# Feed-forward up-projections of a hybrid decoder step: blocks of two by two in seven products

## The chip, the cores and the metric

One Trainium2 chip, one core. The metric is the device time of one launch in microseconds (us), the median of several runs. PE is TensorE (matmuls), PEld its weight loads, DVE is VectorE, ACT is ScalarE, POOL is GpSimd, SP is SyncE (it issues the loads here).

## What is computed

One step of two layers over 512 prompt tokens and 64 sample tokens, model width 1024, all in float32. Each layer is a mixer (pools and a gated delta rule in the first, a short gated convolution in the second) and a gated feed-forward of width 2816. The change is in the feed-forward:

```python
def conv_ffn(h, buf, w_up, conv_w, w_down):
    up = h @ w_up
    gate, val = up[..., :D_FF], up[..., D_FF:]
    gc, new_buf = causal_dwconv(gate, buf, conv_w)   # 3 taps
    return (jax.nn.silu(gc) * val) @ w_down, new_buf
```

`h` is the RMS norm of `x` with a weight per channel; its factor per token is applied behind the product.

## The kernel before, in words

Activations lie with channels on the partitions: 8 tiles of 128 channels by 2 halves of 288 columns (256 prompt tokens and 32 sample tokens each). Every float32 product is made of three: an operand is split into a rounded high part and a low part (the rest), and PE adds high x high, high x low and low x high in one accumulation. `gemm` (L212) does that for one tile of 128 outputs: for each k-tile of 128 channels six matmuls of 288 columns, three for each half of the tokens (L227, L229, L231), into an accumulator of two PSUM banks (`acc2`, two of them).

`Feed` (L76) brings the weights in the order of use: a DMA from SP into `raw` (two buffers of 128 x 1024), the high part by ACT (L111), the low part by DVE (L113; for some tiles of the first mixer by POOL), into `wh` and `wl` (two buffers each). `get` (L117) keeps it as far ahead as the buffers allow.

`ffn` (L1044) runs in two halves of 11 tiles of the feed-forward width. For each tile: the gate product of 8 k-tiles (48 matmuls), `ext_mul` (L260, L262) scales it into `e`, which has two earlier columns in front and the states of the samples (`ext_halo`, `ext_state`: POOL copies at L249, L266, L267); `conv` (L269) is one tap on ACT (L271) and two on DVE (L273); silu on ACT (L1062); times `rE`, the norm's factor, on DVE (L1063). Then the value product (48 matmuls), the gated product by `ext_to_t` (L279, L281), and `split_hl` makes its high part on ACT (L284) and its low part on DVE (L285) in `gh`, `gl`. After 11 tiles come the 8 down products, each over 11 k-tiles, added to `x` by `residual` (L343).

At the end of a product that makes a new `x`, `norm_operand` (L287) makes the split operand of the next one and `norm_sum` (L293) adds up squares; `norm_end` (L317) runs from a hook after five k-steps of the next product and puts two small matmuls for each half into PE's queue. `last` (L1085) does the last two down products by halves of the tokens.

The order on each engine is not written out: a scheduler orders the instructions by their place in the program and by when their operands are ready in its own reckoning, and gives out buffers and semaphores; on the chip each engine then runs its list in that fixed order.

Of the kernel before, what the change touches and what calls it, by code (L numbers as in the profile page):

```python
# [8 lines left out]
F = mybir.dt.float32  # L9
R = mybir.dt.float32r  # L10
# [7 lines left out]
KD = D // 128  # L18
# [56 lines left out]

class Feed:  # L76
    """Weights of the products in the order in which they are used: loaded ahead and split into two parts."""

    def __init__(self, tc, pool, units):
        self.tc, self.nc, self.pool, self.units = tc, tc.nc, pool, units  # L80
        self.raw, self.hl = {}, {}
        self.nd = self.ns = self.n = 0
        self.between = None
        self.slow = ()

    def cuts(self, i, w):
        """the first in halves, for an early start"""
        return ((0, 512), (512, w)) if i == 0 else ((0, w),)

    def load(self, upto):  # L90
        while self.nd < min(upto, len(self.units)):
            src, w = self.units[self.nd]
            t = self.pool.tile([128, 1024], F, tag="raw", name="raw", bufs=RAWB)
            for a, b in self.cuts(self.nd, w):
                self.nc.sync.dma_start(out=t[:, a:b], in_=src[:, a:b])
                if self.between and self.nd == 0 and a == 0:
                    self.between()
            self.raw[self.nd] = t
            self.nd += 1

    def split(self, upto):
        while self.ns < min(upto, len(self.units)):
            self.load(self.ns + 1)
            t = self.raw.pop(self.ns)
            w = self.units[self.ns][1]
            if self.ns < len(self.units) - 2:
                h, l = (self.pool.tile([128, 1024], R, tag=n, name=n, bufs=HLB) for n in ("wh", "wl"))
            else:
                h, l = (self.extra.tile([128, 768], R, tag=n, name=n, bufs=2) for n in ("eh", "el"))
            for a, b in self.cuts(self.ns, w):  # L110
                self.nc.scalar.activation(out=h[:, a:b], in_=t[:, a:b], func=AF.Copy)  # L111
                e = self.nc.gpsimd if self.ns in self.slow else self.nc.vector
                e.tensor_tensor(out=l[:, a:b], in0=t[:, a:b], in1=h[:, a:b].bitcast(F), op=SUB)  # L113
            self.hl[self.ns] = (h, l)
            self.ns += 1

    def get(self):  # L117
        i = self.n
        self.n += 1
        self.split(i + HLB)  # L120
        self.load(i + HLB + RAWB)
        return self.hl.pop(i)
# [10 lines left out]
LY = (4, 8)  # L133
# [8 lines left out]
RAWB, HLB, WB = 2, 2, 6  # L142


def body(ctx, tc, I, O):
# [9 lines left out]
    wk = pool(ctx, "wk")  # L155
    xm = pool(ctx, "xm")
    ps = pool(ctx, "ps", space=PSUM)

    cst = com.tile([128, NCST], F, name="cst")
    vec = com.tile([128, NVEC], F, name="vec")  # L160

    def C(name, rows=128):
        o, w = CST[name]
        return cst[0:rows, o:o + w]
# [9 lines left out]
    def W(name="w"):  # L174
        return wk.tile([128, 711], F, tag="w", name=name, bufs=WB)
# [7 lines left out]
    units = []  # L183
    for c in ORD.split():
        if c != "g":
            units.append((I["w_in_ab"][{"p": 0, "q": 4, "k": 8, "v": 12, "z": 16}[c[0]] + int(c[1])], 1024))
    for m in range(8):
        units.append((I["w_out_ab"][m], 1024))

    def ffn_units(l):  # L190
        for half in range(2):
            for f in range(half * HF, half * HF + HF):
                units.append((I["w_up"][l, f], 1024))
                units.append((I["w_up"][l, NF + f], 1024))
            for m in range(8):
                k0 = half * HF
                units.append((I["w_down"][l, m][:, k0 * 128:(k0 + 6) * 128], 768))
                units.append((I["w_down"][l, m][:, (k0 + 6) * 128:(k0 + 11) * 128], 640))

    ffn_units(0)  # L200
    for m in range(8):
        for j in (1, 2, 0):
            units.append((I["w_in_c"][j * 8 + m], 1024))
    for m in range(8):
        units.append((I["w_out_c"][m], 1024))
    ffn_units(1)
    feed = Feed(tc, wts, units)
# [3 lines left out]
    # ---------------------------------------------------------------- pieces  # L211
    def gemm(out, H, L, kmap, nks):  # L212
        """out[:, c] (+)= W.T @ x over the k-tiles of one accumulation, in the order kmap; nks: k-tiles per unit"""
        tot = sum(nks)
        oc = out if isinstance(out, list) else [out[:, 0], out[:, 1]]
        i = k0 = 0
        for nk in nks:
            h, l = feed.get()
            for _ in range(nk):
                k = kmap[i]  # L220
                kk = k - k0
                wh = h[:, kk * 128:(kk + 1) * 128]
                wl = l[:, kk * 128:(kk + 1) * 128]
                st, sp = i == 0, i == tot - 1
                xh, xl = (H[k], L[k]) if isinstance(H, list) else (H[:, k], L[:, k])
                for c in range(2):
                    PE.matmul(out=oc[c][:, 0:288], lhsT=wh, rhs=xh[:, c, :], start=st, stop=False)  # L227
                for c in range(2):
                    PE.matmul(out=oc[c][:, 0:288], lhsT=wh, rhs=xl[:, c, :], start=False, stop=False)  # L229
                for c in range(2):  # L230
                    PE.matmul(out=oc[c][:, 0:288], lhsT=wl, rhs=xh[:, c, :], start=False, stop=sp)  # L231
                i += 1
                yield
            k0 += nk
# [16 lines left out]
    def ext_mul(e, h, a, b):  # L251
        """e's data columns = a * b, both [128, 2, >=288] by token columns"""
# [24 lines left out]
    def ext_to_t(dst, c, h, b):  # L277
        """dst [128, 2, 288] = outputs of a convolution (columns of c) * b"""
# [8 lines left out]
    def norm_operand(x, xh, xl, k, nw):  # L287
        """x [128, 2, 288] * w, split: the operand of the next product but for the factor of a token"""
# [28 lines left out]
    def norm_end(rE=None):  # L317
        h = wk.tile([128, 576], R, tag="w", name="acch", bufs=WB)
        l = wk.tile([128, 576], R, tag="w", name="accl", bufs=WB)
# [25 lines left out]
    # ---------------------------------------------------------------- start: operand and norm of the first layer  # L345
    xwh = ops.tile([128, KD, 2, 288], R, tag="xh", name="xwh")
    xwl = ops.tile([128, KD, 2, 288], R, tag="xl", name="xwl")
# [15 lines left out]
    feed.load(1)  # L363
    start(3)
    feed.load(2)
    start(KD)
    nc.sync.dma_start(out=cst, in_=I["cst"])
    for k in range(KD):
        norm_operand(xs[k], xwh, xwl, k, ("nmix", 0))
        feed.split(min(k + 1, 2))  # L370
# [4 lines left out]
    # ---------------------------------------------------------------- first mixer: pools and gated delta  # L375
# [6 lines left out]
    late = pool(ctx, "late")  # L382
# [956 lines left out]
```

## Time and profile before

| | |
|---|---|
| median of 3 runs | 1386.51 us (1386.44 to 1387.59) |
| span of the profiled execution, first to last instruction | 1381.5 us |
| median less span | 5.0 us |
| matmuls (all, with the small ones) | 9996 |
| granted TensorE clock, mean | 0.977 |

The profile is one execution on one core. The time of that execution is listed nowhere by itself; in the sums its own time is taken as its span and the 5.0 us around it. A line of the groups reads: source line, engine, operation, output <- inputs by tile name, shapes, count, busy time, mean of one in ns, idle time before it and what ended that. The timeline reads: start in us, duration in us, engine, line, operation, and in brackets the idle time before it with its releaser. A matmul's duration is its whole passage, and the next one starts before it ends; the pace is read from the starts or from the count.

### The profile page before, as it was taken

Reading aid. Unit: us, or ns where it says so; the run is one execution under the profiler, and the core shown is the slowest. Engines: PE = TensorE matmul, PEld = TensorE weight load, DVE = VectorE, ACT = ScalarE, POOL = GpSimd, SP = SyncE. Lnnn points to the kernel's source line nnn. Section 1 sums busy time; section 2 is a strip of 40 time slices with the busy share of each in tenths; the row PEclk is TensorE's granted clock in tenths of the full one; section 3 lists DMA queues with packets and bytes.
Section 4 is the critical chain, followed back from the end, with each engine's and each line's share of the span. In section 5 each row is a group of like instructions: output and inputs, shape, how many; then the busy total and the mean of one; then the engine's idle time right before and its main releaser. Section 6 shows DMA issues by size and latency. Waiting matters only on the chain.

```text
span 1381.5 us, 23767 instructions
## 1 busy us (share of the span) xinstructions
PE 1348.7 (98%) x9996; PEld 1325.1 (96%) x9996; DVE 760.6 (55%) x1260; ACT 500.1 (36%) x781; POOL 174.0 (13%) x316
## 2 busy tenths in 40 slices
PE   8898999899999999999999999999999999999997
PEld 7788789899999999999999999999999999999997
DVE  7669537986555324555446454456655423555434
ACT  6463326655333212333334222234333212333333
POOL 2123112201111001111000011000111000111000
PEclk9889779999999999999999999999999999999999
DMA  5111122362222232222232222222222233222232
GB/s 200 43 40 59 40 62 76 98 191 84 77 92 74 73 85 92 92 77 82 81 84 98 80 77 92 79 85 84 77 92 79 74 84 102 77 82 88 70 84 90
DMA packets 51081, 117.37 MB, mean 85 GB/s; under 512 B 5280, under 2 KB 22048, under 8 KB 50976
## 3 DMA queue, kind: packets, MB, share of 16 engines
q1 hardware_dynamic: 50976, 115.87, 26.3%
q8 instruction: 78, 1.28, 0.4%
q14 instruction: 27, 0.22, 0.1%
HBM read 110.21 MB, written 5.64 MB: 84 GB/s over the span
## 4 chain that ended last, share of the span: by engine, by line
PE 87%; DVE 8%; ACT 3%; issue 2%; DMA 0%; SPq 0%; POOLq 0%; POOL 0%; ACTq 0%
PE mm L231 27%; PE mm L227 27%; PE mm L229 27%; DVE c L273 2%; PE mm L1108 1%; DVE Xb L690 1%; DVE tm L688 1%; PE kqs L925 1%; PE mp L731 0%; PE up L867 0%; PE kk L649 0%; ACT xwh L290 0%; ACT wh L111 0%; DMA x<-in_x_dram 0%; DVE t L311 0%
## 5 line engine op out<-in xcount | busy, mean ns | idle before, releaser
L111 ACT ACTIVATE wh<-raw 128x1024 fp32r<-128x1024 f32 (+2 forms) x211 | 206.1, 977 | 613.3 <-PE mm L229 553.1
L227 PE MATMUL mm<-xh,wh 128*128 128x288 f32 x1792 | 382.7, 295 | 0.0
L231 PE MATMUL mm<-xh,wl 128*128 128x288 f32 x1792 | 382.7, 295 | 0.0
L229 PE MATMUL mm<-xl,wh 128*128 128x288 f32 x1792 | 382.4, 295 | 0.0
L227 PEld LDWEIGHTS mm<-xh,wh 128*128 128x128 f32 x1792 | 288.0, 188 | 0.2 <-issue 0.2
L231 PEld LDWEIGHTS mm<-xh,wl 128*128 128x128 f32 x1792 | 288.0, 188 | 0.0
L229 PEld LDWEIGHTS mm<-xl,wh 128*128 128x128 f32 x1792 | 288.0, 188 | 0.0
L113 DVE TENSOR_TENSOR wl<-raw,wh 128x1024 fp32r<-128x1024 f32 (+2 forms) x193 | 214.4, 1111 | 110.1 <-ACT wh L111 105.7
L231 PE MATMUL mm<-gh,wl 128*128 128x288 f32 x788 | 169.2, 296 | 0.0
L229 PE MATMUL mm<-gl,wh 128*128 128x288 f32 x788 | 169.1, 296 | 0.0
L227 PE MATMUL mm<-gh,wh 128*128 128x288 f32 x788 | 169.1, 296 | 0.0
L227 PEld LDWEIGHTS mm<-gh,wh 128*128 128x128 f32 x788 | 127.3, 189 | 0.0
L231 PEld LDWEIGHTS mm<-gh,wl 128*128 128x128 f32 x788 | 127.3, 189 | 0.0
L229 PEld LDWEIGHTS mm<-gl,wh 128*128 128x128 f32 x788 | 127.3, 189 | 0.0
L273 DVE SCALAR_TENSOR_TENSOR c<-e,vec,c 128x592 f32<-128x592 f32 (+1 forms) x140 | 121.7, 872 | 7.7 <-ACT c L271 5.4
L260 DVE TENSOR_TENSOR e<-mm,rT 128x512 f32<-128x512 f32 x59 | 40.7, 691 | 152.9 <-PE mm L231 152.4
L266 POOL COPY nfp<-e 128x2 f32<-128x2 f32 x44 | 11.3, 257 | 629.9 <-DVE e L260 629.9
L227 PE MATMUL mm<-xwh,wh 128*128 128x288 f32 x304 | 77.5, 330 | 6.4 <-ACT wh L111 6.4
L229 PE MATMUL mm<-xwl,wh 128*128 128x288 f32 x304 | 77.3, 329 | 0.0
L231 PE MATMUL mm<-xwh,wl 128*128 128x288 f32 x304 | 77.1, 329 | 0.0
L279 DVE TENSOR_TENSOR g<-c,mm 128x512 f32<-128x512 f32 x52 | 35.8, 688 | 63.3 <-PE mm L231 63.2
L227 PEld LDWEIGHTS mm<-xwh,wh 128*128 128x128 f32 x304 | 55.5, 209 | 7.2 <-ACT wh L111 6.7
(362 smaller groups left out, 1457.6 us busy)
## 6 DMA issues: line engine op xcount, KB each, us to landing
raw<-in_w_up_dram SPq DMA_DIRECT2D x88, 512.0 KB, 3.2
raw<-in_w_down_dram SPq DMA_DIRECT2D x32, 384.0 KB, 3.1
raw<-in_w_in_c_dram SPq DMA_DIRECT2D x24, 512.0 KB, 3.2
raw<-in_w_down_dram SPq DMA_DIRECT2D x32, 320.0 KB, 2.9
raw<-in_w_in_ab_dram SPq DMA_DIRECT2D x19, 512.0 KB, 3.2
hss<-in_state_dn_dram SPq DMA_DIRECT2D x16, 256.0 KB, 3.0
raw<-in_w_out_ab_dram SPq DMA_DIRECT2D x8, 512.0 KB, 3.4
raw<-in_w_out_c_dram SPq DMA_DIRECT2D x8, 512.0 KB, 3.2
```

Source lines behind the costliest of these rows:

```text
L111: self.nc.scalar.activation(out=h[:, a:b], in_=t[:, a:b], func=AF.Copy)
L113: e.tensor_tensor(out=l[:, a:b], in0=t[:, a:b], in1=h[:, a:b].bitcast(F), op=SUB)
L227: PE.matmul(out=oc[c][:, 0:288], lhsT=wh, rhs=xh[:, c, :], start=st, stop=False)
L229: PE.matmul(out=oc[c][:, 0:288], lhsT=wh, rhs=xl[:, c, :], start=False, stop=False)
L231: PE.matmul(out=oc[c][:, 0:288], lhsT=wl, rhs=xh[:, c, :], start=False, stop=sp)
L260: V.tensor_tensor(out=P2(e[:, h:h + PT]), in0=a[:, :, 0:256], in1=b[:, :, 0:256], op=MUL)
L273: V.scalar_tensor_tensor(out=c[:, 0:n], in0=e[:, j:j + n], scalar=vcol(vname, idx * (h + 1) + j), in1=c[:, 0:n], op0=MUL, op1=ADD)
L279: V.tensor_tensor(out=dst[:, :, 0:256], in0=P2(c[:, 0:PT]), in1=b[:, :, 0:256], op=MUL)
L688: V.tensor_tensor(out=tv, in0=lv.to_broadcast([128, a, b]), in1=xv.to_broadcast([128, a, b]), op=MUL)
L690: V.tensor_tensor(out=uv, in0=uv, in1=tv, op=ADD)
L925: PE.matmul(out=kq[:, h * 128:(h + 1) * 128], lhsT=km[:, b].rearrange("p i t -> p (i t)"), rhs=t[:, s], start=b == 0, stop=b == 7)
L1108: PE.matmul(out=o[m][:, c, 0:288], lhsT=a[:, w], rhs=b[:, k, c], start=k == i == 0, stop=k == HF - 1 and i == 2)
```

## The change

The up-projection of a feed-forward tile is taken as a product of blocks: rows gate and value (128 outputs each), inner dimension in two halves of 4 k-tiles, columns in the two halves of the tokens. Seven products of sums of blocks take the place of eight. Weight sums (`add`) are made on GpSimd, four additions of 128 x 512 for a tile; the sums of activations (`form_operand`) on VectorE when the operand is made, with their split. A tile thus has the weight units raw (1024 columns), two sums (1024 each) and a half block (512, its low part on GpSimd). The products are chained through two PSUM banks and a third (`b`), with copies to SBUF by ACT in between; the last two products of a tile run among those of the next (`sevens`). `Gated` has the work behind the products: half of the gate's scaling and the product with `rE` go to GpSimd, the state copies to ACT. The feed-forward runs in three passes of 8, 7 and 7 tiles instead of two of 11, and out projections make their tiles in the order 0 4 1 5 2 6 3 7. The number of buffers changes from the feed-forward on: 4 `raw`, 3 pairs of `wh` and `wl`, 2 pairs of 512 columns, 3 of sums, 7 work tiles of 594 columns; some tiles of the mixer and the constants move to other places.

```diff
 class Feed:
...
+    def pairs(self, srcs):
+        prev = None
+        for t in [*srcs, None]:
+            if t is not None:
+                r, g = len(self.loads), len(self.groups)
+                self.loads += [(t[0], 1024, 4), (t[1], 1024, 3)]
+                self.groups.append(r)
+                self.plan += [("raw", r, 1024), ("sum", g, 1)]
+            if prev is not None:
+                self.plan.append(("one", prev + 1, 512))
+            if t is not None:
+                self.plan.append(("sum", g, 0))
+                prev = r
...
+    def add(self):
+        g = self.ng
+        if g == len(self.groups) or self.groups[g] + 1 >= self.nl or self.sgs.places() < 2:
+            return False
...
+        add = lambda out, x, y: self.nc.gpsimd.tensor_tensor(out=out, in0=x, in1=y, op=ADD)
+        add(t0[:, lo], b[:, lo], b[:, hi])
+        add(t1[:, lo], t0[:, lo], a[:, lo])
+        add(t1[:, hi], a[:, lo], b[:, lo])
+        add(t0[:, hi], t1[:, lo], a[:, hi])
...
+    def split(self):
...
+        for a, b in self.cuts(self.ns, w):
+            self.nc.scalar.activation(out=h[:, a:b], in_=src[:, a:b], func=AF.Copy)
+            e = self.nc.gpsimd if kind == "one" or kind == "raw" and n in self.slow else self.nc.vector
+            e.tensor_tensor(out=l[:, a:b], in0=src[:, a:b], in1=h[:, a:b].bitcast(F), op=SUB)
...
+    def ahead(self):
+        while self.load() or self.add() or self.split():
+            pass
...
+RAWX, HLX, HL1, SGB, WX = 2, 1, 2, 3, 7
+PASS = ((0, 8), (8, 7), (15, 7))
+PAIR = (0, 4, 1, 5, 2, 6, 3, 7)
...
+    def sevens(tiles, ops):
+        fa, fb, ft = ops
+        x11, x21, x22 = ([t[:, i] for i in range(2)] for t in (fa, fb[:, :, :, 0], fb[:, :, :, 1]))
+        d1, t3, d2, t4 = ([ft[:, i, :, n] for i in range(2)] for n in range(4))
+
+        def product(o, u, half, x, first, last):
+            h, l = u[2:]
+            xh, xl = x
+            for j in range(4):
+                w = slice(half * 512 + j * 128, half * 512 + j * 128 + 128)
+                for i, (a, b) in enumerate(((h, xh), (h, xl), (l, xh))):
+                    PE.matmul(out=o[:, 0:288], lhsT=a[:, w], rhs=b[:, j], start=first and j == i == 0,
+                              stop=last and j == 3 and i == 2, skip_group_check=True)
+                yield
+        prev = None
+        for t in [*tiles, None]:
+            if t is not None:
+                o, b, sv = acc2(), bank("b"), W("sv")
+                p, q = o[:, 0], o[:, 1]
+                t.begin()
+                u = feed.take()
+                yield from product(p, u, 0, x11, True, False)
+                S.activation(out=sv[:, 0:288], in_=p[:, 0:288], func=AF.Copy)
+                yield from product(b, u, 1, x21, True, True)
+                feed.done(u)
+                t.c11(sv[:, 0:288], b[:, 0:288])
+            if prev is not None:
+                was, p0, q0, sv0, u = prev
+                yield from product(p0, u, 1, x22, False, True)
+                feed.done(u)
+                was.c12(p0[:, 0:288])
+            if t is not None:
+                u1 = feed.take()
+                yield from product(p, u1, 0, d2, False, False)
+                S.activation(out=sv[:, 288:576], in_=p[:, 0:288], func=AF.Copy)
+            if prev is not None:
+                u = feed.take()
+                yield from product(q0, u, 0, t4, False, True)
+                feed.done(u)
+                was.c21(sv0[:, 288:576], q0[:, 0:288])
+            if t is not None:
+                yield from product(q, u1, 1, t3, True, False)
+                feed.done(u1)
+                u = feed.take()
+                yield from product(p, u, 0, d1, False, False)
+                t.c22(p[:, 0:288], q[:, 0:288])
+                prev = (t, p, q, sv, u)
...
+    def form_operand(x, F3, m, nw, half):
...
+        S.activation(out=P2(xw[:, 0:576]), in_=x, func=AF.Copy, scale=w)
+        j = m % 4
+        if m < 4:
+            S.activation(out=fa[:, 0, j], in_=xw[:, 0:288], func=AF.Copy)
+            V.tensor_tensor(out=fa[:, 1, j], in0=xw[:, 0:288], in1=fa[:, 0, j].bitcast(F), op=SUB)
+            half[j] = xw
+            return
+        S.activation(out=fb[:, 0, j], in_=P2(xw[:, 0:576]), func=AF.Copy)
+        V.tensor_tensor(out=fb[:, 1, j], in0=P2(xw[:, 0:576]), in1=fb[:, 0, j].bitcast(F), op=SUB)
...
+        for i in range(2):
+            d = W("fd")
+            d1, t = d[:, 0:288], d[:, 288:576]
+            if i == 0:
+                V.tensor_tensor(out=d1, in0=y[:, 0:288], in1=y[:, 288:576], op=SUB)
+                V.tensor_tensor(out=t, in0=xw[:, 288:576], in1=y[:, 288:576], op=SUB)
+                d0 = d1
+            else:
+                V.scalar_tensor_tensor(out=d1, in0=d0, scalar=-1.0, in1=xw[:, 288:576], op0=MUL, op1=SUB)
+                V.scalar_tensor_tensor(out=t, in0=d1, scalar=-1.0, in1=xw[:, 0:288], op0=MUL, op1=SUB)
+            split_hl(ft[:, 0, j, 2 * i:2 * i + 2], ft[:, 1, j, 2 * i:2 * i + 2], P2(d[:, 0:576]))
...
+    class Gated:
...
+        def half(self, on, c, a):
+            e = self.e
+            es = smp(e[:, 2 + PT:2 + PT + 80], 2)
+            on.tensor_tensor(out=e[:, 2 + 256 * c:258 + 256 * c], in0=a[:, 0:256], in1=rT[:, c, 0:256], op=MUL)
+            on.tensor_tensor(out=es[:, c, :, 2:10], in0=a[:, 256:288].rearrange("p (s t) -> p s t", s=4),
+                             in1=rT[:, c, 256:288].rearrange("p (s t) -> p s t", s=4), op=MUL)
+        def c11(self, a, b):
+            V.tensor_tensor(out=self.v[:, 0:288], in0=b, in1=a, op=ADD)
+            self.half(G, 0, self.v[:, 0:288])
+        def c12(self, a):
+            self.half(V, 1, a)
+            e = self.e
+            c = self.c = W("c")
+            n = conv(e, c, 2, "cff", self.l * 66 // 3 + self.f)
+            S.activation(out=self.sp[:, self.f], in_=e[:, PT:PT + 2], func=AF.Copy)
+            S.activation(out=self.ss[:, self.f], in_=self.es[:, :, 8:10], func=AF.Copy)
+            S.activation(out=c[:, 0:n], in_=c[:, 0:n], func=AF.Silu)
+            G.tensor_tensor(out=c[:, 0:n], in0=c[:, 0:n], in1=rE[:, 0:n], op=MUL)
+        def c22(self, a, b):
+            S.activation(out=self.v[:, 288:576], in_=a, func=AF.Copy, scale=-1.0)
+            V.tensor_tensor(out=self.v[:, 288:576], in0=self.v[:, 288:576], in1=b, op=SUB)
+        def c21(self, a, b):
+            V.scalar_tensor_tensor(out=self.v[:, 0:288], in0=b, scalar=-1.0, in1=a, op0=MUL, op1=SUB)
...
+            ext_to_t(P2(t[:, 0:576]), self.c, 2, v)
+            split_hl(*self.g, P2(t[:, 0:576]))
...
     def ffn(l, nw):
...
-        for half in range(2):
+        for f0, n in PASS:
             gh, gl = gtiles()
...
+            yield from sevens([Gated(l, f0 + j, st, sp, ss, gh, gl, j) for j in range(n)], ops_)
...
+                yield from gemm(o, gh, gl, range(n))
```

## Rows read from the trace of the kernel before

**Rows 1.** The page, busy time, share of the span and instructions of each engine.
```profile
PE 1348.7 (98%) x9996; PEld 1325.1 (96%) x9996; DVE 760.6 (55%) x1260; ACT 500.1 (36%) x781; POOL 174.0 (13%) x316
```
**Rows 2.** The page, the chain that ended last, by engine.
```profile
PE 87%; DVE 8%; ACT 3%; issue 2%; DMA 0%; SPq 0%; POOLq 0%; POOL 0%; ACTq 0%
```
**Rows 3.** Windows: busy us (count) of PE, PEld, DVE, ACT, POOL; clock, DMA share, GB/s.
```profile
400.00:500.00 100.00, 100.00 (x752) 100.00 (x752) 44.81 (x62) 27.44 (x34) 10.51 (x20) 1.00 0.26 79
440.72:453.50 12.78, 12.78 (x98) 12.78 (x97) 7.15 (x10) 4.30 (x5) 2.16 (x4) 1.00 0.21 58
```
**Rows 4.** Timeline of DVE behind two results of the last product.
```profile
1354.26 0.46 DVE L1111 TENSOR_TENSOR xr<-xr,mm 128x288 f32<-128x288 f32 x1 [1.16 <-PE mm L1108]
...
1358.66 0.45 DVE L1111 TENSOR_TENSOR xr<-xr,mm 128x288 f32<-128x288 f32 x1 [2.43 <-PE mm L1108]
```
**Rows 5.** Groups of instructions, shapes apart: POOL, DVE, ACT.
```profile
L113 POOL TENSOR_TENSOR wl<-raw,wh 128x1024 fp32r<-128x1024 f32 x18 | 43.2, 2402 | 113.8 <-ACT wh L111 77.0 <-PE mm L231 30.3 <-ACT Vb_s L759 6.5
L1164 POOL TENSOR_TENSOR y<-xr,rb 128x288 f32<-128x288 f32 x2 | 1.6, 792 | 83.8 <-ACT rb L1163 83.8
...
L113 DVE TENSOR_TENSOR wl<-raw,wh 128x1024 fp32r<-128x1024 f32 x129 | 158.0, 1225 | 21.2 <-ACT wh L111 16.7 <-issue 0.2
L273 DVE SCALAR_TENSOR_TENSOR c<-e,vec,c 128x592 f32<-128x592 f32 x104 | 86.5, 832 | 3.9 <-ACT c L271 1.8
L285 DVE TENSOR_TENSOR gl<-g,gh 128x576 fp32r<-128x576 f32 x52 | 39.1, 752 | 4.5 <-ACT gh L284 4.5
L279 DVE TENSOR_TENSOR g<-c,mm 128x512 f32<-128x512 f32 x52 | 35.8, 688 | 63.3 <-PE mm L231 63.2
L281 DVE TENSOR_TENSOR g<-c,mm 128x64 f32<-128x64 f32 x52 | 11.4, 220 | 1.6
...
L111 ACT ACTIVATE wh<-raw 128x1024 fp32r<-128x1024 f32 x147 | 155.7, 1059 | 418.2 <-PE mm L229 373.5 <-issue 44.3 <-PE mm L231 0.2
L271 ACT ACTIVATE c<-e,vec 128x592 f32<-128x592 f32 x52 | 41.2, 792 | 5.4 <-DVE e L262 1.3
L284 ACT ACTIVATE gh<-g 128x576 fp32r<-128x576 f32 x52 | 35.7, 687 | 14.2 <-DVE g L281 7.9
L1062 ACT ACTIVATE c<-c 128x592 f32<-128x592 f32 x44 | 30.8, 699 | 84.6 <-DVE c L273 84.5
L290 ACT ACTIVATE xh<-x,vec 128x576 fp32r<-128x576 f32 x12 | 9.3, 775 | 2.7 <-DVE x L1019 1.4 <-DVE x L343 1.2
```
**Rows 6.** Timeline of DVE, two places in the first mixer, one in the feed-forward.
```profile
57.19 2.17 DVE L601 TENSOR_TENSOR t<-t,t 128x20 f32<-128x20 f32 x1
59.39 0.18 DVE L602 TENSOR_TENSOR t<-t 128x20 f32<-128x20 f32 x1
...
133.91 0.75 DVE L454 TENSOR_TENSOR z<-mm,rT 128x576 f32<-128x576 f32 x1
...
441.82 1.23 DVE L113 TENSOR_TENSOR wl<-raw,wh 128x1024 fp32r<-128x1024 f32 x1
```
**Rows 7.** Timeline of POOL at the same places, and one tile later.
```profile
56.93 2.39 POOL L113 TENSOR_TENSOR wl<-raw,wh 128x1024 fp32r<-128x1024 f32 x1 [13.80 <-ACT wh L111]
...
133.88 2.37 POOL L113 TENSOR_TENSOR wl<-raw,wh 128x1024 fp32r<-128x1024 f32 x1 [6.47 <-ACT Vb_s L759]
...
441.83 1.28 POOL L267 COPY nfs<-e 128x16 f32<-128x16 f32 x1
...
455.42 0.19 POOL L267 COPY nfs<-e 128x16 f32<-128x16 f32 x1
```
**Rows 8.** Window 115 to 120 us, columns as in rows 3.
```profile
115.00:120.00 5.00, 5.00 (x28) 5.00 (x27) 4.93 (x9) 1.13 (x3) 3.42 (x5) 0.66 0.29 89
```
**Rows 9.** Timeline of PE around a wait in the first mixer.
```profile
114.03 0.66 PE L754 MATMUL vp<-cst,vf 128*128 128x128 f32 x4 [1.93 <-ACT vf L435]
...
115.92 0.69 PE L227 MATMUL mm<-xwh,wh 128*128 128x288 f32 x2
116.40 0.69 PE L229 MATMUL mm<-xwl,wh 128*128 128x288 f32 x2
```

More of the change, by code (lines that the diff above doesn't have):

```diff
@@ L73, in constants, with __init__, add, pick @@
     return c
-class Feed:
[L79 to L82, printed above, removed]
+class Slots:
+    def __init__(self):
+        self.tags, self.left, self.n = [], {}, 0
+    def add(self, make, bufs):
+        self.tags.append((make, bufs, []))
+    def pick(self):
+        best = None
+        for make, bufs, had in self.tags:
+            old = had[-bufs] if len(had) >= bufs else -1
+            if (old < 0 or self.left[old] == 0) and (best is None or old < best[0]):
+                best = (old, make, had)
+        return best
+    def free(self):
+        return self.pick() is not None
+    def places(self):
+        n = 0
+        for _, bufs, had in self.tags:
+            n += max(0, bufs - len(had))
+            for old in had[-bufs:]:
+                if self.left[old]:
+                    break
+                n += 1
+        return n
+    def take(self, uses):
+        _, make, had = self.pick()
+        had.append(self.n)
+        self.left[self.n] = uses
+        self.n += 1
+        return self.n - 1, make()
+    def used(self, i):
+        self.left[i] -= 1
+        assert self.left[i] >= 0
@@ L101, in split @@
[L101 to L115, printed above, removed]
@@ new lines, in split @@
+    def split(self):
+        if self.ns == len(self.plan):
+            return False
+        kind, n, w = self.plan[self.ns]
+        places = self.one if kind == "one" else self.hls
+        if not places.free() or (kind != "sum" and n >= self.nl) or (kind == "sum" and (n, w) not in self.sums):
+            return False
+        if kind == "sum":
+            (i, src), w = self.sums[n, w], 1024
+            self.sgs.used(i)
+        else:
+            i, src = self.raw[n]
+            src = src[:, 512:1024] if kind == "one" else src
+            self.raws.used(i)
+        at, (h, l) = places.take(1)
+        for a, b in self.cuts(self.ns, w):
+            self.nc.scalar.activation(out=h[:, a:b], in_=src[:, a:b], func=AF.Copy)
+            e = self.nc.gpsimd if kind == "one" or kind == "raw" and n in self.slow else self.nc.vector
+            e.tensor_tensor(out=l[:, a:b], in0=src[:, a:b], in1=h[:, a:b].bitcast(F), op=SUB)
+        self.hl[self.ns] = (places, at, h, l)
+        self.ns += 1
+        return True
@@ L119, in get, with take, done @@
+    def ahead(self):
+        while self.load() or self.add() or self.split():
+            pass
+    def take(self):
+        self.ahead()
         self.n += 1
-        self.split(i + HLB)
-        self.load(i + HLB + RAWB)
-        return self.hl.pop(i)
+        return self.hl[self.n - 1]
+    @staticmethod
+    def done(x):
+        x[0].used(x[1])
 CY = [2, 3, 3]
@@ L1095, in last @@
         o = {m: acc2() for m in (6, 7)}
-        parts = {m: [feed.get(), feed.get()] for m in (6, 7)}
+        parts = {m: feed.take()[2:] for m in (6, 7)}
         v, r, t = (gp_.tile([128, 2, 3], F, name=n) for n in ("fv", "fr", "ft"))
```

272 lines of the change are left out of this document (150 added, 122 removed).

## The prediction

> **What bounds the kernel now.** I read the page first: PE is busy for 98% of the span, DVE for 55%, ACT for 36%, POOL for 13% [rows 1]. Busy shares are averages, so the chain that ended last comes next; PE holds 87% of it [rows 2]. Then the busy time by windows, for the stage that is changed. In 400 to 500 us PE runs 752 matmuls without a pause at full clock, 0.133 us each; and in one feed-forward tile (12.78 us, 96 matmuls) DVE is busy for 7.15 us, ACT for 4.30, POOL for 2.16 [rows 3]. So the stage is bound by the number of matmuls, and DVE has 5.6 us of slack in each tile. All 44 tiles (22 in each of two layers) take 44 x 12.78 = 562 us.
>
> **What is removed.** Seven products of 4 k-tiles and 3 parts are 84 matmuls where there were 96: 12 x 44 = 528 fewer, 528 x 0.133 = 70 us. A product now writes one bank 12 times in a row and changes weights at each matmul. The last product does that already: between two of its results lie 4.40 us for 33 matmuls, 0.133 each [rows 4]. So the rate stays, and a tile costs PE 84 x 0.133 = 11.17 us.
>
> **What is added, by engine.** Durations are from the groups by shape [rows 5]. A POOL tensor_tensor takes 2.40 us for 1024 columns and 0.79 for 288, so 0.16 + 0.0022 per column (an estimate from these two): 1.28 for 512, 1.46 for 592, 0.72 for 256.
> - POOL, for each tile: four adds of 512, the low part of the half block of 512, half of the gate product (256 and 32 columns), the product c * rE (592). That is 5 x 1.28 + 0.72 + 0.23 + 1.46 = 8.8 us. The state copies of before leave it.
> - DVE: three low parts of 1024 instead of two (3.68 us), two convolution taps (1.66), the gated product (0.91), its low part (0.75), all as before but one; and four steps of 288 columns at 0.46 [rows 4] with two tails, some 2.0. The c * rE leaves. Sum 9.0 us.
> - ACT: three high parts of 1024 (3.18), one of 512 (half of 1.06, and a little), three copies of 288 out of PSUM (some 1.3), first tap 0.79, silu 0.70, high part 0.69, three small state copies (0.6): 7.8 us.
> Each by itself is below PE's 11.17 us. The DMA engines move the same up-projection weights, two loads of 512 KB for a tile; SP issues 24 down loads for a layer instead of 32. At a DMA share of 0.26 [rows 3] I cost that at nothing: the loads hide behind the tile before, and were that cover gone, POOL's adds would start late.
>
> **But POOL and DVE do not run beside each other.** Here the timelines decide. At 57.19 a DVE product over 20 columns took 2.17 us, while the next one of that size took 0.18 [rows 6]; it ended when POOL's 2.39 us subtraction ended, that had begun at 56.93 [rows 7]. The other way round, POOL's copy of 16 columns at 441.83 took 1.28 us beside DVE's 1.23 us subtraction, and 0.19 at 455.42 without one [rows 6, 7]. What these DVE instructions share is two inputs in SBUF. One with an input in PSUM is not stopped: z<-mm,rT took its 0.75 us at 133.91 under POOL's 2.37 [rows 6, 7]. So one of the two holds the way into SBUF for a whole instruction and the other waits. How long: the 20 columns were let go at 59.36 - 0.18 = 59.18, 2.25 after POOL's start, so a hold is 0.14 shorter than the duration; DVE's hold was 1.28 - 0.19 + 0.01 = 1.10 of 1.23, the same.
> The Trainium skill has this as a rule (SBUF — State Buffer, "Who interferes with whom"): the shared port pair is an exclusive lock, taken by a DVE instruction with two SBUF inputs against a GpSimd instruction that reads SBUF, and one with at most one SBUF input does not contend. The trace agrees in both halves; without the rule's second half the tile below would be 15.7 us and not 13.7.
>
> Holds in a tile: POOL 5 x 1.14 + 0.58 + 0.10 + 1.32 = 7.7 us. DVE with two SBUF inputs: 3 x 1.10 + 2 x 0.70 + 0.56 + 0.09 + 0.62 = 6.0. Sum **13.7 us** against PE's 11.17, and against 12.78 now. The four short steps read PSUM and fit under POOL. So the shared way becomes the bound of the up-projections, not PE.
>
> **The sum of the stage.** 44 x 13.7 = 603 us. From that goes what lies outside the stage, six times (three passes in each layer): the four adds and two low parts of a pass's first tile, done under the down products before it (4.56 + 2.2), and the end of its last tile, done under those after it (1.4 + 1.32 + 0.65 + 0.62): 10.75 x 6 = 64. That leaves 539, if the way is never free. It will be free at times: within a tile the users wait for ACT, between taps and c * rE for the first tap and silu (0.79 + 0.70), and at the end for the high part (0.69). No row of before shows how much of that other tiles fill. The bounds are 0 and 2.2 us a tile; I take 1.5, the first two, since these sit between users of the way in one tile while the adds of the next cover the third. 15.2 x 44 - 64 = 605, **+43** on 562. The bounds give 539 (-23) and 15.9 x 44 - 64 = 636 (+74); with the four short steps exclusive too (15.7 + 2.2), 724 (+162).
>
> **Ends of the passes**, six instead of four. After the last x22 product the gate runs through half of e (0.6), first tap, two taps (1.66), silu, c * rE (1.46), gated product (0.91), high and low part (0.69 + 0.75): 7.6 us. PE has one product (1.6) and n - 1 of n k-steps of the first down product (0.80 each: 4.8 or 5.6): 6.4 to 7.2. Now it is 2.35 us against ten steps, 8 us. In that moment the first adds of the next pass stand in POOL's queue, and c * rE waits behind one. There is also a wait of its own: the x22 product goes on in the bank that ACT has just begun to copy, with no product of a next tile between, 0.4 to 1.5 us. I take 2.5 us each, +15; 0 to 5 is the bound.
>
> **Starts of the two feed-forwards.** After the last output tile DVE adds the residual (0.75, as the other steps of 576 columns), ACT weights it (0.78), DVE makes two differences (0.9), ACT and DVE split them (0.69 + 0.75), and again (0.9 + 0.69 + 0.75), with another split between (0.75): 7 us to the last form, while PE has two and three quarters products, 4.4. Now: 2.3 us against seven k-steps (5.6). +2.6 each, and the norm's sum is read after 2 us instead of 4: I take +3 each, **+6**, bounds 0 and 12. The new places of A, Y and the constants I cost at nothing: their users are done while the out projection runs, and were they late, the first forms would wait for them.
>
> Sum: -70 from PE is not collected; +43 +15 +6 = +64. The profiled execution has a span of 1381.5 us, the median of the runs is 1386.5; the 5.0 us around the span stay. 1386.5 + 64 = **1450 us**.
>
> **Rivals.**
> - *PE stays the bound* (faster). The point that decides: the holds of POOL and DVE stay under 11.2 us a tile. For it: each engine's own sum does. Against: 13.7 from rows, both ways of blocking seen. -70 + 15 = 1331 us. Chance 0.08.
> - *The way is full all the time and only it counts* (faster). Weights are prepared up to a product ahead, so queues may never run dry: 539 in place of 562, with little at the ends (+6): 1370 us; up to 1384. Against: fixed order in each queue. Chance 0.12.
> - *The waits come in lumps and the clock falls* (much slower). Granted clock 0.66 in 115 to 120 us [rows 8], after PE had waited 1.93 us: pairs of matmuls then stood 0.48 us apart [rows 9] instead of 2 x 0.133. A mean of 0.66 is 5 x 0.34 / 0.5 = 3.4 us at the lower of the two levels (1.2 GHz), which loses 1.7 us. If the sums come late by one such lump in each tile: 44 x 1.7 = 75, 1525 us. It decides if PE's lost time at the lower clock no longer fits under the way's 13.7. Chance 0.14.
>
> **How the numbers follow.** The forecast's own case, 1389 to 1500, has 0.62; 0.04 is left for within 0.2% (2.8 us, about what a measurement of this kernel can tell from no change). Faster 0.08 + 0.12 = 0.20, slower 0.62 + 0.14 = 0.76. The range leaves out the first rival and the upper part of the third: 1370 to 1530.
>
> **What would show it.** Right: up-projection tiles of 14 to 16 us with PE idle 3 to 4 us in each, waiting for ACT and DVE splits; POOL's 512-column adds and DVE's subtractions stretched well past 1.28 and 1.23, in turns; POOL busy over half of the stage; down products still at 752 matmuls in 100 us. Wrong: tiles of 11.2 us with PE unbroken, or adds that run beside DVE's subtractions without either stretching. Tiles above 17 us, with a granted clock below 1, speak for the third rival.

## The result, and the profile after

The changed kernel takes 1453.15 us (1452.43 to 1453.82), the kernel before 1386.47 us beside it: 1.048 of the time, interval 1.0463 to 1.0493, so 66.7 us slower. The profiled execution has a span of 1450.6 us, 69.1 more than the one of before. The page, busy time by engine, and the first line of the chain that ended last:

```profile
PE 1320.0 (91%) x9468; PEld 1270.9 (88%) x9468; DVE 967.1 (67%) x1440; ACT 639.7 (44%) x1149; POOL 595.1 (41%) x536
...
PE 3%; DVE 1%; issue 1%; ACT 0%; POOL 0%; POOLq 0%; ACTq 0%
```

The 528 matmuls are gone, yet PE is busy for only 28.7 us less than in [rows 1], as waits and a lower clock stretch what is left, and it is idle for 131 us of the span instead of 33. The chain breaks off early here (its shares add up to 5%, against 87% for PE alone in [rows 2]), so stages were read instead. Each runs from its first matmul to that of the next; behind the changed up-projections the boundary is where the down products go on alone, since 14 or 16 of their matmuls run among the last up-projections of a pass:

| stage | before, us | after, us |
|---|---|---|
| first mixer, products in | 251.2 | 245.9 |
| its output product | 60.7 | 62.4 |
| up-projections of layer 0 | 141.6 + 140.8 | 131.3 + 95.8 + 95.9 |
| up-projections of layer 1 | 138.3 + 140.8 | 122.6 + 95.2 + 97.9 |
| second mixer with its output product | 205.9 | 205.4 |
| down products and end | 295.8 | 292.2 |

The up-projections went from 561.5 to 638.6 us, +77. The rest came out 8 us shorter. Of these 5.3 are the first mixer's, which differs about that much between the profiles of kernels that leave it alone (245.9 to 250.5 us in the changed kernel and its variants, 248.8 to 251.2 in the kernel before and its variants). Another 3.6 are the down products', and only because 88 of their matmuls, 11.7 us at 0.133 each, now count with the up-projections.

Windows of the changed kernel, columns as in [rows 3]: one tile of the first pass, one of the second, a pass of seven tiles, and a stretch at the start of each feed-forward:

```profile
375.51:390.76 15.25, 11.92 (x84) 11.22 (x84) 12.88 (x14) 7.04 (x14) 11.80 (x10) 1.00 0.23 70
...
516.25:530.44 14.19, 11.91 (x84) 11.22 (x85) 11.53 (x13) 7.05 (x14) 12.23 (x10) 1.00 0.23 74
...
496.09:591.87 95.78, 84.28 (x605) 80.34 (x603) 72.64 (x88) 48.18 (x88) 66.39 (x51) 1.00 0.23 73
...
325.00:335.00 10.00, 7.11 (x27) 6.41 (x28) 5.97 (x4) 5.13 (x8) 9.92 (x8) 0.51 0.39 126
...
985.00:995.00 10.00, 7.89 (x36) 7.17 (x36) 6.19 (x11) 5.56 (x9) 1.37 (x2) 0.66 0.17 55
```

A tile took 12.78 us in [rows 3]. In the middle of a pass it now takes 14.2 in four of the six passes and 14.9 to 15.2 in the other two, the first of layer 0 and the last of layer 1. In the first tile shown, 15.25 long, PE's 84 matmuls fill 11.92, DVE is busy for 12.88 and POOL for 11.80. In a pass POOL is busy for 69% of the time. No engine is full, and yet the tile is as long as it is. Groups by shape, DVE first, show a sign of the cause:

```profile
L223 DVE TENSOR_TENSOR wl<-raw,wh 128x1024 fp32r<-128x1024 f32 x101 | 152.6, 1510 | 16.8 <-ACT wh L221 13.8
L470 DVE SCALAR_TENSOR_TENSOR c<-e,vec,c 128x592 f32<-128x592 f32 x104 | 131.7, 1266 | 4.0 <-ACT c L468 2.5
L223 DVE TENSOR_TENSOR wl<-sg,wh 128x1024 fp32r<-128x1024 f32 x88 | 129.6, 1473 | 17.6 <-ACT wh L221 16.4
...
L194 POOL TENSOR_TENSOR sg<-sg,raw 128x512 f32<-128x512 f32 x88 | 148.7, 1689 | 97.9 <-issue 87.7 <-DVE wl L223 9.8
L194 POOL TENSOR_TENSOR sg<-raw 128x512 f32<-128x512 f32 x88 | 139.1, 1586 | 148.3 <-DMA raw<-in_w_up_dram 144.6 <-ACT v L1280 3.5 <-issue 0.2
```

The low parts of 1024 columns took 1225 ns in [rows 5] and take 1473 to 1510; a tap went from 832 to 1266 ns; POOL's adds of 512 columns, 1.28 us when nothing stops them, average 1.59 and 1.69. The busy times contain waiting. The timeline of DVE and POOL in the first of these tiles shows for what:

```profile
377.17 3.33 DVE L470 SCALAR_TENSOR_TENSOR c<-e,vec,c 128x592 f32<-128x592 f32 x2
...
382.81 1.77 DVE L476 TENSOR_TENSOR e<-c,v 128x512 f32<-128x512 f32 x1 [1.95 <-POOL c L1277]
384.50 1.21 DVE L223 TENSOR_TENSOR wl<-sg,wh 128x1024 fp32r<-128x1024 f32 x1
...
385.77 0.44 DVE L1281 TENSOR_TENSOR v<-v,mm 128x288 f32<-128x288 f32 x1
386.60 1.45 DVE L482 TENSOR_TENSOR gl<-e,gh 128x576 fp32r<-128x576 f32 x1 [0.39 <-ACT gh L481]
...
377.80 0.79 POOL L1262 TENSOR_TENSOR e<-v,rT 128x32 f32<-128x32 f32 x1
378.56 1.30 POOL L223 TENSOR_TENSOR wl<-raw,wh 128x512 fp32r<-128x512 f32 x1
...
381.31 1.47 POOL L1277 TENSOR_TENSOR c<-c,rE 128x592 f32<-128x592 f32 x1 [0.28 <-ACT c L1276]
382.73 1.29 POOL L194 TENSOR_TENSOR sg<-raw 128x512 f32<-128x512 f32 x1
386.13 1.29 POOL L194 TENSOR_TENSOR sg<-sg,raw 128x512 f32<-128x512 f32 x1 [2.10 <-issue]
```

POOL's add at 382.73 ends at 384.02; the DVE product that stood at 382.81 ends 0.56 later, what is left of it. Then DVE has the way: its subtraction at 384.50 takes an unhindered 1.21 us. POOL stands still meanwhile. The profile names no releaser ("issue"); that its next add waits for this subtraction, to write the buffer that it reads, is inferred: the add starts 0.42 us behind its end here, and 0.13 to 0.14 in four other tiles. `gl` at 386.60 is stopped again. In between, at 385.77, the step that reads PSUM takes 0.44 us, as in [rows 4]. Adding up the time in which one of POOL's reading instructions or one of DVE's with two SBUF inputs runs, from the timelines, gives the time in which the shared way is in use: 14.15 us of the first tile shown, 15.25 long, and 67.9 of 70 in the stretch of 510 to 580 us. In most of the steady tiles, 14.2 us apart, it is free for 0.03 to 0.04 us (0.46 in the last of them in a pass); in the two slower passes for 0.8 to 1.1.

What PE waits for, from its waits (us in total, times, longest):

```profile
PE mm L363 <- DVE v L1281: 46.8, 38, 4.4
PE mm L363 <- DVE e L1262: 18.7, 27, 1.1
PE mm L363 <- DVE v L1284: 8.8, 24, 0.6
...
PE mm L340 <- ACT gh L481: 5.4, 6, 0.9
```

The steps of DVE named are short ones that read PSUM; they come late since DVE's queue in front of them does, as the run with own banks below bears out.

### The profile page after: what moved, and what is told of

Same layout as the page of the kernel before. It is cut to its first block, busy times and chain, and to the rows that moved or that the text cites. A ratio compares the mean times of both kernels' runs of the same rounds, so it can differ in the third digit from the quotient of the medians.

```text
span 1450.6 us, 23564 instructions
## 1 busy us (share of the span) xinstructions
PE 1320.0 (91%) x9468; PEld 1270.9 (88%) x9468; DVE 967.1 (67%) x1440; ACT 639.7 (44%) x1149; POOL 595.1 (41%) x536
## 3 DMA queue, kind: packets, MB, share of 16 engines
q8 instruction: 74, 1.21, 0.3%
## 5 line engine op out<-in xcount | busy, mean ns | idle before, releaser
L363 PE MATMUL mm<-ft,wh 128*128 128x288 f32 x1408 | 293.9, 303 | 27.7 <-DVE e L1262 18.7
L363 PEld LDWEIGHTS mm<-ft,wh 128*128 128x128 f32 x1408 | 231.3, 193 | 36.2 <-DVE e L1262 25.3
L363 PE MATMUL mm<-ft,wl 128*128 128x288 f32 x704 | 210.8, 299 | 0.8 <-DVE wl L223 0.8
L194 POOL TENSOR_TENSOR sg<-raw 128x512 f32<-128x512 f32 x88 | 139.1, 1586 | 148.3 <-DMA raw<-in_w_up_dram 144.6
L194 POOL TENSOR_TENSOR sg<-sg,raw 128x512 f32<-128x512 f32 x88 | 148.7, 1689 | 97.9 <-issue 87.7
L223 POOL TENSOR_TENSOR wl<-raw,wh 128x512 fp32r<-128x512 f32 (+1 forms) x62 | 103.1, 1662 | 114.3 <-ACT wh L221 80.7
L223 DVE TENSOR_TENSOR wl<-sg,wh 128x1024 fp32r<-128x1024 f32 x88 | 129.6, 1473 | 17.6 <-ACT wh L221 16.4
L363 PEld LDWEIGHTS mm<-ft,wl 128*128 128x128 f32 x704 | 135.6, 193 | 1.4 <-DVE wl L223 1.4
L363 PE MATMUL mm<-fb,wh 128*128 128x288 f32 x352 | 79.1, 317 | 46.8 <-DVE v L1281 46.8
L221 ACT ACTIVATE wh<-sg 128x1024 fp32r<-128x1024 f32 x88 | 92.8, 1054 | 64.6 <-PE mm L342 26.9
```

Of the source, the lines that this page charges most:

```text
L194: add = lambda out, x, y: self.nc.gpsimd.tensor_tensor(out=out, in0=x, in1=y, op=ADD)
L221: self.nc.scalar.activation(out=h[:, a:b], in_=src[:, a:b], func=AF.Copy)
L223: e.tensor_tensor(out=l[:, a:b], in0=src[:, a:b], in1=h[:, a:b].bitcast(F), op=SUB)
L363: PE.matmul(out=o[:, 0:288], lhsT=a[:, w], rhs=b[:, j], start=first and j == i == 0, stop=last and j == 3 and i == 2, skip_group_check=True)
```

## The experiments

Two theories stand against each other. **The shared way**: POOL's instructions and DVE's with two SBUF inputs exclude each other, and the sum of their holds bounds a tile. **Hops or banks**: the tile is bound by the order of steps between engines, or by PSUM, whose first bank waits for a reader of the second (`c22`, L1281, the longest wait above).

The kernel before had medians of 1383.5 to 1386.5 us beside these runs, so a difference between rows is sure to about 3 us. The ratios are each against the runs beside it.

| run | us | against before | tile in the steady passes, us |
|---|---|---|---|
| changed kernel | 1453.2 | 1.048 | 14.2 (15 in two passes) |
| adds twice | 1658.7 | 1.199 [1.1965, 1.2013] | 20.6 (18 to 20 in two passes) |
| memsets in place of adds | 1368.3 | 0.989 [0.987, 0.9909] | 11.6 to 12.1 |
| adds on VectorE | 1392.6 | 1.007 [1.0054, 1.0086] | 12.65 |
| own banks | 1448.8 | 1.047 [1.0454, 1.0489] | 14.2 |
| adds on VectorE, own banks | 1395.6 | 1.008 [1.0062, 1.0096] | 13.0 |
| three of four adds on VectorE, own banks | 1415.1 | 1.022 [1.0205, 1.0242] | 13.2 |
| before with 4 more adds | 1391.2 | 1.005 [1.0031, 1.0058] | 12.8 |
| before with 8 more adds | 1447.6 | 1.046 [1.0439, 1.0481] | 14.6 |
| factor behind the down products | 1389.3 | 1.003 [1.0018, 1.0042] | 12.7 |
| that, and adds on VectorE | 1344.7 | 0.971 [0.9688, 0.9733] | 11.3 |
| before, factor behind the down products | 1387.3 | 1.001 [0.9996, 1.0021] | 12.8 |

**Adds twice.** Each add is made a second time, with the same result.

```diff
-        add(t0[:, lo], b[:, lo], b[:, hi])
...
+        for _ in range(2):
+            add(t0[:, lo], b[:, lo], b[:, hi])
...
```

> The four weight additions of each tile are done twice on GpSimd (the same result). Theory (the way into SBUF that POOL and DVE share is full): 4 x 1.14 = 4.6 us more of holds in each tile, for the 38 tiles that are not the first of a pass: +175 us and up to +200, 1630 to 1655 us. Rival 1 (PE waits because DVE's short reads of PSUM stand behind long instructions, by order and by banks): DVE's list is the same, less than +60, below 1510. Rival 2 (POOL's own time brings the sums late): POOL goes from 8.8 to 13.9 us a tile, still under the tile's 15.2; less than +60, below 1510.

Measured 205.5 us above the changed kernel, a little over the upper end: 4.67 us a tile on the average, where four holds of 1.14 make 4.56. That this is so near is in part luck. The steady tiles came 20.6 apart, 6.4 more: the way is in use for about 4.8 us more in each and free for 1.4 to 1.8, POOL waits for a DMA of `raw` (1.47 us in the tile from 580.61), and the mean granted clock fell (0.903 in all). The tiles at the borders paid less. Three tiles of that kernel:

```profile
580.61:642.67 62.06, 41.38 (x254) 40.70 (x253) 35.69 (x39) 21.42 (x39) 51.27 (x39) 0.78 0.16 50
```

Both rivals fall: they allowed 60 us at most.

**Memsets in place of adds.** The sums of weights are left as zeros.

```diff
-        add(t0[:, lo], b[:, lo], b[:, hi])
...
+        for _ in range(2):
+            self.nc.gpsimd.memset(t0, 0.0)
+            self.nc.gpsimd.memset(t1, 0.0)
```

> The four weight additions of each tile are left out: four memsets of 1024 columns on GpSimd stand in their place (they write SBUF and read nothing), so the sums of weights are zero. POOL's time for them is nearly the same, 4 x 0.95 = 3.8 us instead of 5.1. Theory: the holds fall from 13.7 to 9.1 us a tile, below PE's 11.17; tiles of 11.2 to 11.8 us, stage 515 to 540 us instead of 639: 1330 to 1355 us. Rival 1: DVE's list is unchanged, so at most the 1.3 us a tile that POOL saves, not under 1395. Rival 2: the same bound, POOL only saves 1.3 us a tile: 1395 to 1453.

Measured 1368.3, 13 us over the theory's range, far below the rivals'. As many instructions on POOL, a quarter shorter (0.96 us for 1.28) and without reading SBUF, let the tile fall to 11.6 to 12.1 us:

```profile
505.45:517.53 12.08, 11.65 (x87) 11.19 (x86) 8.74 (x13) 7.17 (x13) 8.47 (x10) 1.00 0.28 89
```

The shorter instructions save POOL 1.3 us a tile, and the tile fell by 2.1 to 3.4; so it is the adds' reading that costs. The 13 us are mostly at the starts: first passes of 108.5 and 104.7 us where a pass of seven and one more tile, 85.7 + 12.1 = 97.8, would fit, though no add is waited for.

**Adds on VectorE.**

```diff
-        add = lambda out, x, y: self.nc.gpsimd.tensor_tensor(out=out, in0=x, in1=y, op=ADD)
+        add = lambda out, x, y: self.nc.vector.tensor_tensor(out=out, in0=x, in1=y, op=ADD)
```

> The four weight additions of each tile move from GpSimd to VectorE; all is computed. Theory: an addition of 512 columns holds the way 0.56 us on DVE and 1.14 on POOL, so the holds fall from 13.7 to 11.4 us a tile; DVE's own time rises from 9.0 to 11.8 and becomes the bound: tiles of 12 to 12.6 us, 1370 to 1395 us. Rival 1: DVE's list gets four instructions longer, its short reads of PSUM come later still: 1453 or more. Rival 2: the sums come earlier, as in the theory.

1392.6, as expected: 60.6 us less for one word. VectorE makes an add in 0.77 to 0.83 us with its waits, less than the 1.14 for which POOL's holds the way. What is left of POOL's work still stops it, as its groups show:

```profile
L194 DVE TENSOR_TENSOR sg<-raw 128x512 f32<-128x512 f32 x88 | 71.8, 827 | 25.4 <-DMA raw<-in_w_up_dram 25.3
L194 DVE TENSOR_TENSOR sg<-sg,raw 128x512 f32<-128x512 f32 x88 | 68.2, 774 | 0.2
...
L476 DVE TENSOR_TENSOR e<-c,v 128x512 f32<-128x512 f32 x44 | 30.5, 692 | 70.2 <-POOL c L1277 70.2
```

The gated product waits 70.2 us, 1.6 in each tile, for POOL's c * rE. The way is free for 0.63 us of a steady tile here, so it is no longer the way's sum alone that sets the 12.65.

**Own banks.** The second accumulator gets a bank of its own, so that no wait for `c22` can come from it.

```diff
-                p, q = o[:, 0], o[:, 1]
+                p, q = o[:, 0], bank("q")
```

> The second accumulator of a tile (q) becomes a PSUM tile of its own, so that a product into the first need not wait for a read of the second. Theory: the waits on those reads go, but the holds remain 13.7 to 14.2 us a tile and PE waits elsewhere: 1435 to 1455 us. Rival 1: the 46.8 and 18.7 us that PE waited for DVE v and DVE e are the loss: 1388 to 1400 us. Rival 2: no change, 1453.

The longest wait of all falls from 46.8 to 4.4 us (on `q`, by itself now), and the time stays: 1.047 of before in place of 1.048. PE's waits in this kernel:

```profile
PE mm L363 <- ACT sv L375: 58.5, 30, 6.6
PE mm L363 <- ACT v L1280: 15.6, 24, 1.2
```

They have a new name and the old size. The rival of the banks falls: the wait was where the delay came to light.

**Both of these**, and then **three of the four adds on VectorE** (the first one on POOL again):

> Both edits together: the weight additions on VectorE and the second accumulator as a PSUM tile of its own. Theory (holds first; once they are under DVE's time, the waits on short reads of PSUM count): with the additions on DVE, PE still waited 23 us for DVE e and 9 for DVE v; these go, tiles fall from 12.65 to about 12.0 us: 1365 to 1380 us, below the kernel before. Rival (as with the holds full, the waits only move): 1388 to 1393 us.

> As the run before, but the first of the four additions stays on GpSimd. Theory: holds 11.4 + 0.6 = 12.0 us a tile, DVE's own time 11.8 - 0.7 = 11.1: the way is the bound again, tiles of 12.0 to 12.6 us; the same as all four on VectorE or up to 15 us slower. Rival (DVE's own time is what counts now): up to 20 us faster.

Both missed. The first: 1395.6, no gain from the banks with the adds on VectorE either, and 2.6 us above the rival's range. The second: one add back on POOL costs 19.5 us, 0.44 a tile, where the theory allowed up to 15 and tiles of at most 12.6 (they came 13.25 apart); the direction is the theory's, and freeing VectorE of an add does not help. The way is free for 0.32 us of a steady tile in both.

**Adds put into the kernel before.** Each up-projection tile gets 4 or 8 adds of 512 columns on GpSimd, into a tile that nobody reads (the first tiles of layer 0 go without). All else stays: the products and their banks. A tile has two weight units; with four adds each makes two, with eight, as shown, four.

```diff
+            if self.ns in self.extra_adds and hasattr(self, "extra"):
+                d = self.extra.tile([128, 512], F, tag="dum", name="dum", bufs=1)
+                for _ in range(4):
+                    self.nc.gpsimd.tensor_tensor(out=d, in0=t[:, 0:512], in1=t[:, 512:1024], op=ADD)
             self.hl[self.ns] = (h, l)
...
```

> The kernel before, with the same four GpSimd additions of 512 columns in each feed-forward tile, into a tile that nobody reads. Theory: DVE's holds there are 2 x 1.10 + 1.4 + 0.7 + 0.65 + 0.62 = 5.6 us a tile, with 4.6 for the additions 10.2, under PE's 12.78: no change, within 4 us of before, though single DVE subtractions are stretched. Rival (GpSimd work beside DVE costs time by itself): +40 us or more.

> The kernel before, with eight such additions in each feed-forward tile. Theory: 5.6 + 9.1 = 14.7 us of holds a tile against PE's 12.78; 44 x 1.9 = +85 us, less what falls under the down products (two units of each of four halves): +60 to +100 us. Rival (GpSimd's own time, 10.2 us a tile, is still under 12.78): no change.

Four adds cost 5.9 us, 1.9 more than expected, eight 62, as expected. That is the bound by a maximum: DVE's holds in a tile of before are about 5 us (an estimate from [rows 5]: 2 x 1.10 + 2 x 0.70 + 0.62, and as much again for c * rE, a step of that size; the two expectations counted 0.7 more for the gated product, which reads PSUM there). With four adds 5 + 4.6 = 9.6 stays under PE's 12.78; with eight, 5 + 9.1 = 14.1 does not, and behind the first tiles of a half the tiles came 14.6 apart. A window of the kernel with four adds, and one of that with eight:

```profile
540.00:660.00 120.00, 120.00 (x902) 120.00 (x901) 88.84 (x95) 40.67 (x48) 77.92 (x74) 1.00 0.25 84
```

```profile
560.00:700.00 140.00, 131.24 (x951) 128.22 (x950) 98.34 (x98) 40.09 (x49) 135.45 (x113) 0.99 0.21 71
```

In the first DVE is stretched (88.84 us of 120, where [rows 3] have 44.81 of 100) and PE never pauses; where the 5.9 us lie is not shown, since the profiled run was the fastest of its kernel (1386.7 us). In the second POOL is busy for 97%, with adds that stand in line: in one tile, from the timeline, one of the two users runs for 14.55 of 14.63 us. Nothing uses what the adds make; the delay gets to PE since POOL's copies into `e` stand in its queue behind them, and ACT's tap waits for these copies (us in total, times, longest, in the same 140 us):

```profile
ACT c L280 <- POOL e L258: 53.0, 9, 6.5
```

By its own time POOL would not be late: eight adds of 1.28 and the short copies are about 11 us a tile (an estimate from [rows 5] and [rows 7]), under 12.78. It is late for what DVE holds.

**The factor behind the down products.** By the theory any hold that leaves a tile brings its length. The norm's factor per token is the same for all channels, so c * rE can leave the tiles; the down products carry it, where DVE has time.

```diff
     def residual(x, o, m):
-        V.tensor_tensor(out=x[m], in0=x[m], in1=o[:, :, 0:288], op=ADD)
+        y = W("yr")
+        V.tensor_tensor(out=P2(y[:, 0:576]), in0=o[:, :, 0:288], in1=rT, op=MUL)
+        V.tensor_tensor(out=x[m], in0=x[m], in1=P2(y[:, 0:576]), op=ADD)
...
             S.activation(out=c[:, 0:n], in_=c[:, 0:n], func=AF.Silu)
-            G.tensor_tensor(out=c[:, 0:n], in0=c[:, 0:n], in1=rE[:, 0:n], op=MUL)
```

(and the same two steps in the last two down products.)

> Edit: the product c * rE on GpSimd (592 columns, once in each of the 44 tiles) is left out; the norm's factor per token is the same for every channel, so the down products can carry it: the step that adds a down product to x first multiplies it by rT (one more VectorE step of 576 columns for each of 24 output tiles of a layer, under the down products). Theory (the way into SBUF, shared by GpSimd and VectorE, bounds a tile): its hold of 1.32 us goes from 14.15 us a tile, 44 x 1.32 = 58 us off 1453, and up to 1 us comes to the end of the last pass: 1390 to 1402 us, tiles of 12.8 to 13.0 us. Rival (the tile is bound by the chain of hops between engines, in which c * rE has slack, or by PSUM banks): 1435 to 1455 us.

> Edit: as the run with the factor moved behind the down products, and the four additions of weights on VectorE instead of GpSimd. Against the run with the additions alone moved (1392.6 us, tiles of 12.65 us). Theory (VectorE waits for GpSimd's holds, 1.32 us of them gone for each tile; VectorE's own time is then 11.3 to 11.8 us a tile, PE's 11.17): tiles of 11.3 to 11.8 us, 44 x 0.85 to 1.35 = 37 to 59 us less, 1333 to 1357 us, faster than the kernel before. Rival (the hops or PSUM banks keep the tile at 12.6 us): 1385 to 1394 us.

> Edit: the kernel before the change with the same factor moved behind its down products (VectorE's product of 592 columns leaves each of 44 tiles, 16 output tiles of a layer get one more of 576). Theory: PE bounds the kernel before and VectorE has 5.6 us of slack in a tile, so no change: within 3 us of the kernel before. Rival (a gain of its own by over 5 us, so that the other two would not speak for the seven products): 1375 us or less.

All three went by the theory, the first 0.7 us below its range. Alone, the edit takes 63.8 us off the changed kernel, 1.45 a tile, a little more than the hold of 1.32; the steady tiles are 12.7 apart and the way is free for 0.03 to 0.04 us in most of them, as before the edit. In the kernel before it does nothing. With the adds on VectorE it gives **1344.7 us, 0.971 of the time before**, the first version that computes everything and is faster than both. There the step that left was both a hold and a result that DVE waited for, so this run does not tell a hold from a hop. One window of a pass and one of about the length of a tile in that kernel:

```profile
471.90:553.80 81.90, 81.72 (x607) 80.50 (x607) 72.83 (x109) 49.34 (x88) 24.69 (x24) 1.00 0.27 82
500.00:511.70 11.70, 11.70 (x89) 11.53 (x88) 11.63 (x18) 7.64 (x14) 4.31 (x4) 1.00 0.30 95
```

PE is busy for 81.72 of 81.90 us: the seven products have become the bound, with DVE (11.63 of 11.70) close behind. Its tiles are 11.3 apart, where the prediction put PE's own time at 11.17.

## Why the prediction was right, and where its terms were off

- **Mechanism and size.** 1450 predicted, 1453.15 measured, most signs on the likeliest branch: steady tiles of 14.2 to 15.2 us, adds and subtractions stretched in turns, POOL busy for over half. Three signs came out otherwise: PE is idle for 2.3 us in most steady tiles, 3.3 in the first one shown, where 3 to 4 were forecast; it waits for short steps that read PSUM and not for splits; and the down products ran at 732 to 734 matmuls in 100 us, not 752. That the time came within 3 us is luck in part: the errors below are larger and cancel. The rule of the Trainium skill that was cited (SBUF — State Buffer, "Who interferes with whom") held in both halves: steps with two SBUF inputs were stretched (832 to 1266 ns), those that read PSUM not (0.44 us).
- **PE, -70 us, not collected.** Right, and shown from the other side: with the way relieved, the fastest kernel collects 41.7 us of it (1386.4 to 1344.7).
- **Holds of 13.7 us a tile.** Measured 14.15, the handing over included: 3% low. c * rE gave 1.45 for the 1.32 put down, and an add about 1.2 for 1.14 in the steady tiles of adds twice.
- **Idle time of the way, 1.5 us a tile.** The amount was right and its place wrong. In most steady tiles of four passes the way is free for 0.03 to 0.04 us: adds and low parts of the next tile fill the gaps left by ACT's tap, silu and high part, as the second rival had it. In the middle of the two slower passes it is free for 0.8 to 1.1. But a whole pass of seven has 9.5 to 11.5 us of it, 1.4 to 1.6 a tile, and these lie at the borders: in the second pass 5.2 in the first tile, where PE never waits, and 4.9 in the last.
- **Borders of the passes.** The prediction took 10.75 us of holds out of each pass and put 2.5 on. Measured in the later passes, with 14.15 a tile: 7 x 14.15 = 99 us of holds, of which 85.2 to 86.4 lie inside, so 13 to 14 lie outside; the idle time above brings the pass to 95.2 to 97.9. By the terms of the prediction it was 7 x 15.2 - 8.2 = 98.2. PE waits 0.9 us for `gh` behind each pass and about 1.0 in front of the last x22 product, near the 2.5 put down for both.
- **Starts of the two feed-forwards, +3 each.** The mis-sized term: 8 x 15.2 - 8.2 + 3 = 116.4 for a first pass; they took 131.3 and 122.6, +15 and +6. Beside a pass of seven and one more tile (95.8 + 14.2 = 110.0) they are 21 and 13 us too long, for the 3 put down: the way is in use for 119.5 and 109.6 us in them, where 85.2 + 14.2 = 99.4 would do, since the first tile's holds lie inside and steps of the norm come on top. Timeline of the first start, PE and POOL:

```profile
322.02 0.82 PE L521 MATMUL nps<-acch,ones_r 128*128 128x288 f32 x2 [3.65 <-ACT acch L481]
...
326.51 0.85 PE L363 MATMUL mm<-ft,wh 128*128 128x288 f32 x2 [2.60 <-ACT wh L221]
...
320.54 0.59 POOL L1240 MEMSET rE<- 128x594 f32 x1 [58.56 <-DVE ft L482]
...
321.12 3.02 POOL L194 TENSOR_TENSOR sg<-raw 128x512 f32<-128x512 f32 x2
```

The prediction counted the steps to the last form and found 7 us (they took 5.6). It passed over the buffers: the tiles of sums and the work tiles of the feed-forward lie in a pool that opens when the mixer's pools close. POOL's first instruction there, a memset that reads nothing, waits until DVE has made the last form (320.34). So the sums of the first tile begin at 321.12 and not under the output product, as the prediction had it when it took the 10.75 off these passes too, and their high part (325.40) comes 7 us after PE has run out of other work. That this wait comes from the place of the buffers is read from the program and the releaser; no run tried other buffers. In the window from 325 us shown above the granted clock is 0.51, the lower level, right behind PE's waits of 3.65 and 2.60 us, which makes the late start cost more. The memset run shows that not all of it is the adds: by the same count about 11 and 7 us of the 21 and 13 were left without them. How these divide between the forms, the norm's matmuls and the buffers was not tried.
- **Sum.** Four later passes -8, two first ones +21, the down products -4, the other stages -4: +5 on the 64, as the two spans say (69.1).
- **Third rival.** Waits in lumps with a falling clock came at the starts of both feed-forwards (0.51 from 325 to 335 us and 0.66 from 985 to 995 in the windows above) and around the third tile of both first passes (0.77 from 350 to 360, 0.83 from 1010 to 1030); in three of the four later passes the clock was 1.00, in the last 0.97.

## What to carry to other kernels

Where GpSimd and VectorE work side by side on SBUF, add up what each holds the way for a unit of work and treat that sum as an engine of its own, beside PE: under PE's time it is nearly free (four adds, 6 us), above it the tile grows to the sum (eight adds, 14.6 us a tile for 12.8, 62 us in all). The cure is to move work off that sum, to the engine with the shorter hold or to a stage where PE covers it, and not to chase the wait with the largest total, which only names the place where the delay comes to light. And when buffers change at a stage's border, ask from when the first tile in the new ones can be written.

## What the runs showed of the hardware that was not expected

The shared way can pack almost without loss: in most steady tiles of four passes of the changed kernel it was free for 0.03 to 0.04 us of 14.2 although it passes between two engines a dozen times in each, in queues of fixed order. It need not: with the adds made twice it stood free for 1.4 to 1.8 us in the steady tiles of the same passes. And moving an add of 512 columns from GpSimd to VectorE saves time even with VectorE the busier engine (60.6 us for 4 x 44 adds, 0.34 us each; back on POOL, one add in four costs 0.44).
